# A gated DeltaNet layer with MLP on one core: down products over eight PSUM banks, up products moved between the token norms

## The chip, the core and the metric

The kernel runs on one core of a Trainium2 chip. The core has four compute engines, each with its own in-order queue of instructions: TensorE (PE: matmuls and transposes; PEld is its weight load), VectorE (DVE), ScalarE (ACT) and GpSimd (POOL). SyncE (SP) and ScalarE issue the DMAs. Engines wait for each other through semaphores. The metric is the device time of one execution in microseconds, and of several runs the median.

## The reference

One layer of a hybrid decoder over 2048 tokens of 1024 float32 features: a gated DeltaNet mixer, then a squared-ReLU MLP with 4096 hidden features, then the final norm.

```python
h = rms_norm(x, norm_mix[0])
x = x + gated_deltanet(h, ...)                       # 8 heads of 128
x = x + squared_relu_mlp(rms_norm(x, norm_mlp[0]), w_up, w_down)
return rms_norm(x, norm_final)

def squared_relu_mlp(h, w_up, w_down):
    return jnp.square(jax.nn.relu(h @ w_up)) @ w_down
```

## The kernel before

**Precision.** A float32 operand is split into a high and a low part. A product is then three matmuls, high by high, low by high and high by low, added up in one PSUM bank: lines 119, 120 and 121 in `dense`. So everything that enters a product is first cast (high) and subtracted (low).

**Stages.** The tokens are handled in two blocks of TB = 1024. Each block goes through the mixer, then `mlp_up`, then `mlp_down`. The tile framework takes the program as written, and its own scheduler decides the order in which each engine gets its instructions; a tile pool with `bufs=n` gives a name n buffers in turn, and whoever wants the next buffer waits for the last reader of what was in it.

**PSUM.** There are eight banks of 128x512 float32. They are shared out in three groups, `banks = dict(pj=3, kq=3, po=2)` (line 86), and `big(tag)` takes the next bank of a group.

**`mlp_up`.** The hidden features are made in tiles of 128 by 1024 tokens. `h2` holds the normalized tokens, features first, in two halves of HB = 512 tokens; the first is there when the stage begins, the second is made here. `part(w, u, hf)` is a plain product: 24 matmuls into a pj bank for one weight tile and one half, then relu and square on ScalarE (lines 742 and 743). Three of them on the first half (lines 761 and 762) stand ahead of the token norms. The norms then take the four tiles of 128 tokens in two pairs (`norm_pair`, loop at 788): VectorE scales a tile (line 218) into half of a `qt` buffer, whose other half a DMA fills with a normalized tile of the first half (`place`, line 772). `sums` (775 to 786) transposes on TensorE into kq banks (`to_features`, line 205, with the cast 207 on ScalarE and the subtraction 208 on VectorE), and makes four differences of quarters on GpSimd (lines 780, 782, 784 and 786), which are transposed too: they feed the fast products (`fast`, 835 to 868), in which seven products of half depth do the work of eight. `qt` has two buffers in its group, but `t4` holds one of them, so that the four tiles of tokens pass through a single one. Line 782 overwrites what the first transposes of a tile read. Behind the norms come the three products on the second half (790) and a fourth pair, then the fast products, which put their results in pj, kq and po banks in turn and write the hidden features to memory.

**`mlp_down`.** Sixteen calls of `down` a block, each for FT = 2 tiles of hidden features. `load(fb)` fetches two tiles u, casts them (uh, line 889, ScalarE) and subtracts (ul, line 890, VectorE, 128x1024 each), and splits two tiles of w_down on GpSimd (lines 92 and 93, called dh and dl or the two halves of w). `down` makes sixteen products, eight tiles of tokens by two halves of the features, of six matmuls each; every product is added to x1 by VectorE (line 915). The load of the next call is written ahead of the products of this one. All the products go to kq banks. The last call of a block adds the final norm (921 to 928) and writes the output through DMAs of two queues. In block 0 the call before the last is interleaved with `first_half`, which normalizes and transposes tokens of the next block through pj banks (lines 182 to 192).

Of the kernel before, what the change touches and what calls it, by code (L numbers as in the profile page):

```python
# [7 lines left out]
F32 = mybir.dt.float32  # L8
# [4 lines left out]
MULT, ADD, SUB = ALU.mult, ALU.add, ALU.subtract  # L13
# [7 lines left out]
TB = 1024  # L21
NT = TB // P
HB = 512
# [10 lines left out]
def tile_kernel(ctx: ExitStack, tc: tile.TileContext, x, w_in, w_out, w_up, w_down, n_mlp, n_fin, consts, out):  # L34
# [3 lines left out]
    pe, act, dve, pool, sp = nc.tensor, nc.scalar, nc.vector, nc.gpsimd, nc.sync  # L38
# [49 lines left out]
    def big(tag):  # L88
        return pp.tile([P, 512], F32, name=tag, tag=tag, bufs=banks[tag])
# [9 lines left out]
    def weights(src, f=1, keep=None):  # L99

        raw = wp.tile([P, D], F32, name="wr", tag="wr", bufs=2)
        sp.dma_start(raw if f == 1 else raw.rearrange("p (f c) -> p f c", f=f), src)
        w2, wh, wl = parts()
        split(wh, wl, raw)
        if keep is not None:
            sp.dma_start(keep, w2.bitcast(F32))
        return wh, wl
# [6 lines left out]
    def dense(ps, lhs, rhs, first=True, last=True):  # L114

        n = len(lhs)
        for i in range(n):
            (ah, al), (bh, bl) = lhs[i], rhs[i]
            pe.matmul(ps, ah, bh, start=first and i == 0, stop=False)  # L119
            pe.matmul(ps, al, bh, start=False, stop=False)  # L120
            pe.matmul(ps, ah, bl, start=False, stop=last and i == n - 1)  # L121

    def half_tiles():
        hh = hp.tile([P, KS, HB], F32R, name="hh", tag="hh")
        hl = hp.tile([P, KS, HB], F32R, name="hl", tag="hl")
        return hh, hl
# [16 lines left out]
    def rstd_of(ssq, use_pool=False):  # L143

        n = ssq.shape[-1]
        m = sm.tile([P, n], F32, name="rm", tag=f"rm{n}")
        dve.tensor_scalar(m, ssq, 1.0 / D, EPS, op0=MULT, op1=ADD)
        r = sm.tile([P, n], F32, name="rst", tag=f"rst{n}", bufs=3)
        if use_pool:
            pool.tensor_tensor(r, m, mhalf, op=ALU.pow)  # L150
        else:
            rsqrt(r, m)
        return r
# [47 lines left out]
    def to_features(ti, src, dst_h, dst_l):  # L201

        ps = big("kq")
        for k in range(4):
            pe.transpose(ps[:, k * P:(k + 1) * P], src[:, k * P:(k + 1) * P], ident)
        p3 = ps.rearrange("p (k t) -> p k t", k=4)
        act.copy(dst_h[:, :, ti], p3)
        dve.tensor_tensor(dst_l[:, :, ti], p3, dst_h[:, :, ti].bitcast(F32), op=SUB)

    def norm_pair(i0, xs, ss, place, nb, hh, hl, sums):  # L210


        ssq = sm.tile([P, 2], F32, name="ssq2", tag="ssq2")
        dve.tensor_reduce(ssq, ss, axis=mybir.AxisListType.X, op=ADD)
        r = rstd_of(ssq)
        for i in range(2):
            xn = place()
            dve.scalar_tensor_tensor(xn, xs[i], r[:, i:i + 1], nb, op0=MULT, op1=MULT)
            ti = slice((i0 + i) * P, (i0 + i + 1) * P)
            for k4 in range(0, KS, 4):  # L220
                to_features(ti, xn[:, k4 * P:(k4 + 4) * P], hh[:, k4:k4 + 4, :], hl[:, k4:k4 + 4, :])
            sums(i0 + i, xn)
# [495 lines left out]
    def mlp_up(blk, o1, x1b, h2a):  # L718
# [6 lines left out]
        with tc.tile_pool(name="mp", bufs=2) as mp:  # L725
# [12 lines left out]
            def u_tile():  # L738
                return wp.tile([P, TB], F32, name="u", tag="xt", bufs=4)

            def relu2(dst, src, r):
                act.activation(r, src, AF.Relu)
                act.activation(dst, r, AF.Square)

            def part(w, u, hf):
                (wh, wl), (hh, hl) = w, h2[hf]
                ps = big("pj")
                dense(ps, [(wh[:, k * P:(k + 1) * P], wl[:, k * P:(k + 1) * P]) for k in range(KS)],
                      [(hh[:, k, :], hl[:, k, :]) for k in range(KS)])
                r = mp.tile([P, HB], F32, name="r", tag="r", bufs=3)  # L750
                relu2(u[:, hf * HB:(hf + 1) * HB], ps, r)
                if hf:
                    return u

            def store(f, u):
                act.dma_start(u_d[f], u)


            ws = [weights(w_up[f]) for f in range(3)]
            us = [u_tile() for f in range(3)]  # L760
            for f in range(3):
                part(ws[f], us[f], 0)
            h2.append(half_tiles())
            t_h = [mp.tile([P, KH, HB], F32R, name=f"th{j}", bufs=1) for j in range(3)]
            t_l = [mp.tile([P, KH, HB], F32R, name=f"tl{j}", bufs=1) for j in range(3)]
# [21 lines left out]

            for i in range(0, HT, 2):
                norm_pair(i, x1b[i:i + 2], ss[i // 2], place, nb, *h2[1], sums)
            for f in range(3):  # L790
                store(f, part(ws[f], us[f], 1))
            w, u = weights(w_up[3]), u_tile()
# [83 lines left out]
    def mlp_down(blk):  # L876

        with tc.tile_pool(name="xp", bufs=1) as xp, tc.tile_pool(name="mq", bufs=2) as mp:
            x1 = [xp.tile([P, D], F32, name=f"x1_{i}") for i in range(NT)]
            nfb = DFF // (P * FT)  # L880

            def load(fb):
                us, ds = [], []
                for j in range(FT):
                    f = fb * FT + j
                    raw = wp.tile([P, TB], F32, name="u", tag="xt", bufs=4)
                    sp.dma_start(raw, u_d[f])
                    uh, ul = [mp.tile([P, TB], F32R, name=n, tag=n, bufs=2 * FT) for n in ("uh", "ul")]
                    act.copy(uh, raw)  # L889
                    dve.tensor_tensor(ul, raw, uh.bitcast(F32), op=SUB)  # L890
                    us.append((uh, ul))
                    raw = wp.tile([P, D], F32, name="wr", tag="wr", bufs=2)
                    sp.dma_start(raw, w_down[f * P:(f + 1) * P, :])
                    if j:
                        _, dh, dl = parts()
                    else:
                        dh, dl = [mp.tile([P, D], F32R, name=n, tag=n) for n in ("dh", "dl")]
                    split(dh, dl, raw)
                    ds.append((dh, dl))
                return us, ds  # L900

            def down(us, ds, last, after=None):
                if last:
                    nfin = mp.tile([P, D], F32, name="nfin", tag="nfin", bufs=1)
                    sp.dma_start(nfin, n_fin.to_broadcast([P, D]))
                for i in range(NT):
                    if last:
                        ssq = sm.tile([P, 2], F32, name="ssqf", tag="ssqf")
                    for nh in range(2):
                        ps = big("kq")  # L910
                        hs = slice(nh * 512, (nh + 1) * 512)
                        dense(ps, [(uh[:, i * P:(i + 1) * P], ul[:, i * P:(i + 1) * P]) for uh, ul in us],
                              [(dh[:, hs], dl[:, hs]) for dh, dl in ds])
                        dst = x1[i][:, hs]
                        dve.tensor_tensor(dst, ps, dst, op=ADD)  # L915
                        if last:
                            y = wp.tile([P, HB], F32, name="yo", tag="xt", bufs=4)
                            act.activation(y, dst, AF.Square, accum_out=ssq[:, nh:nh + 1])
                    if last:
                        m = sm.tile([P, 1], F32, name="mf", tag="mf")  # L920
                        dve.tensor_tensor(m, ssq[:, 0:1], ssq[:, 1:2], op=ADD)
                        r = rstd_of(m, True)
                        r0 = blk * TB + i * P
                        for nh in range(2):
                            hs = slice(nh * 512, (nh + 1) * 512)
                            dve.scalar_tensor_tensor(x1[i][:, hs], x1[i][:, hs], r, nfin[:, hs],
                                                     op0=MULT, op1=MULT)
                            (sp, act)[nh].dma_start(out[r0:r0 + P, hs], x1[i][:, hs])
                    if after:
                        after(i)  # L930

            prev, hT = load(0), None
            for i in range(NT):
                sp.dma_start(x1[i], x1_d[blk * TB + i * P:blk * TB + (i + 1) * P, :])
            for fb in range(1, nfb):
                cur = load(fb)
                after = None
                if fb == nfb - 1 and blk + 1 < nblk:
                    hT = half_tiles()
                    after = first_half(blk + 1, hT)  # L940
                down(*prev, False, after)
                prev = cur
            down(*prev, True)
            return hT

# [82 lines left out]
```

## Time and profile before

| | |
|---|---|
| runs | 2955.99, 2963.18 and 2971.45 us (median 2963.18) |
| the profiled execution | 2953.64 us |
| its span | 2951.9 us |
| mean granted TensorE clock | 0.966 |
| PE, DVE, ACT, POOL busy | 93%, 58%, 36%, 33% of the span |

The profile is a trace of one execution. A row of a timeline has the start in us, the duration in us, the engine, the line of the kernel, the operation, the output and inputs by the program's names, and in brackets how long the engine had been idle and what ended that. A row of a window has its bounds and length, the busy time of PE, PEld, DVE, ACT and POOL with the number of instructions, then the granted TensorE clock as a share of full speed, and the share and rate of the DMA engines. A row of waits has who waited, for whom, the total in us, how often, and the longest. A matmul is shown for longer than the distance to the next one, since they are pipelined: what a matmul costs is read from start to start.

### The profile page before, as it was taken

The page shows a single profiled execution, that of the slowest core. Times are in us where ns is not written, and L with a number is a line of the kernel's source. Part 1 is how long each engine was busy: PE and PEld are TensorE (multiplying, and loading weights), DVE is VectorE, ACT ScalarE, POOL GpSimd, SP SyncE. Part 2 cuts the span into 40 slices and gives each one's busy share as a digit, 9 for nine tenths or more (in the row PEclk, how much of TensorE's full clock was granted, in tenths as well). Part 3 has the DMA queues.
Part 4 walks back from the last instruction along what each step waited for, and adds up shares of the span by engine and source line. Part 5 has one row for each costly group of instructions (what it writes and reads, how often), then busy time and mean ns, then how long its engine had stood idle before and what let it go on. Part 6 is the DMA issues. An engine that isn't in the chain of part 4 may idle for free.

```text
span 2951.9 us, 39239 instructions
## 1 busy us (share of the span) xinstructions
PE 2754.7 (93%) x14376; PEld 2243.1 (76%) x14376; DVE 1710.1 (58%) x3978; ACT 1048.7 (36%) x2382; POOL 961.9 (33%) x790
## 2 busy tenths in 40 slices
PE   7788999999899998999999999999998999999998
PEld 6567778877778886777777778887786888777776
DVE  7887777764422225666688776776442222366666
ACT  3343444443244441000045554545423444200001
POOL 5443222200276763232211111111016766333221
PEclk9898999999999999999999999999998999999999
DMA  6544455566423235222254434435572323522221
GB/s 225 187 164 156 160 193 179 179 216 229 162 100 114 100 114 201 86 86 87 78 179 166 147 131 151 151 136 175 194 245 72 111 103 114 207 93 86 86 92 58
DMA packets 101681, 421.46 MB, mean 143 GB/s; under 512 B 11248, under 2 KB 11504, under 8 KB 79984
## 3 DMA queue, kind: packets, MB, share of 16 engines
q1 hardware_dynamic: 70000, 334.92, 32.9%
q10 hardware_dynamic: 31488, 84.03, 7.8%
q8 instruction: 113, 1.85, 0.3%
q14 instruction: 80, 0.66, 0.1%
HBM read 313.92 MB, written 104.99 MB: 142 GB/s over the span
## 4 chain that ended last, share of the span: by engine, by line
PE 70%; DVE 16%; ACT 5%; issue 5%; POOL 2%; DMA 1%; ACTq 0%; DVEq 0%; POOLq 0%; SPq 0%
PE kq L119 9%; PE kq L121 9%; PE kq L120 9%; PE pj L119 9%; PE pj L121 9%; PE pj L120 9%; DVE c L314 3%; DVE tmp L339 2%; PE po L119 2%; PE po L121 2%; PE po L120 2%; DVE ul L890 1%; DVE tt L341 1%; PE kq L517 1%; PE kq L511 1%
## 5 line engine op out<-in xcount | busy, mean ns | idle before, releaser
L119 PE MATMUL pj<-hh,w 128*128 128x512 f32 x1376 | 562.6, 409 | 0.0
L120 PE MATMUL pj<-hh,w 128*128 128x512 f32 x1376 | 557.1, 405 | 0.0
L121 PE MATMUL pj<-hl,w 128*128 128x512 f32 x1376 | 555.0, 403 | 0.0
L915 DVE TENSOR_TENSOR x<-kq,x 128x512 f32<-128x512 f32 x512 | 347.5, 688 | 267.0 <-PE kq L121 266.2
L121 PEld LDWEIGHTS pj<-hl,w 128*128 128x128 f32 x1376 | 265.1, 193 | 54.2 <-issue 0.4
L119 PEld LDWEIGHTS pj<-hh,w 128*128 128x128 f32 x1376 | 266.0, 193 | 51.7 <-issue 0.7
L120 PEld LDWEIGHTS pj<-hh,w 128*128 128x128 f32 x1376 | 266.3, 194 | 50.3
L314 DVE SCALAR_TENSOR_TENSOR c<-raw,cst,c 128x512 f32<-128x512 f32 x288 | 244.8, 855 | 72.7 <-ACT c L311 60.4
L889 ACT CAST uh<-u 128x1024 fp32r<-128x1024 f32 x64 | 64.1, 1046 | 623.9 <-PE kq L121 573.4
L92 POOL TENSOR_SCALAR w<-wr 128x1024 fp32r<-128x1024 f32 x80 | 86.6, 1082 | 513.2 <-PE po L121 312.9
L119 PE MATMUL kq<-dh,uh 128*128 128x512 f32 x512 | 206.4, 404 | 47.8 <-DVE x L915 40.4
L120 PE MATMUL kq<-dh,ul 128*128 128x512 f32 x512 | 204.7, 400 | 0.8 <-DVE ul L890 0.8
L121 PE MATMUL kq<-dl,uh 128*128 128x512 f32 x512 | 202.2, 395 | 2.8 <-POOL dl L93 2.8
L119 PE MATMUL kq<-w,uh 128*128 128x512 f32 x512 | 204.2, 399 | 0.0
L121 PE MATMUL kq<-w,uh 128*128 128x512 f32 x512 | 204.1, 399 | 0.0
L120 PE MATMUL kq<-w,ul 128*128 128x512 f32 x512 | 202.5, 395 | 0.0
L93 POOL TENSOR_TENSOR w<-wr,w 128x1024 fp32r<-128x1024 f32 x80 | 195.6, 2445 | 4.4
L339 DVE TENSOR_TENSOR tmp<-tt,pr 128x2 f32<-128x2 f32 (+30 forms) x496 | 164.6, 332 | 10.1 <-POOL pr L332 0.5
L92 POOL TENSOR_SCALAR dh<-wr 128x1024 fp32r<-128x1024 f32 x32 | 33.5, 1049 | 400.8 <-PE kq L120 349.6
L119 PEld LDWEIGHTS kq<-dh,uh 128*128 128x128 f32 x512 | 96.5, 189 | 82.8 <-DVE x L915 52.8
L890 DVE TENSOR_TENSOR ul<-u,uh 128x1024 fp32r<-128x1024 f32 x64 | 137.4, 2182 | 5.8 <-ACT uh L889 5.8
L341 DVE TENSOR_REDUCE tt<-tmp 128x1 f32<-128x2 f32 (+30 forms) x496 | 126.1, 254 | 10.0
(372 smaller groups left out, 5577.9 us busy)
## 6 DMA issues: line engine op xcount, KB each, us to landing
w<-wi SPq DMA_DIRECT2D x96, 1024.0 KB, 4.9
wi<-w SPq DMA_DIRECT2D x32, 1024.0 KB, 4.8
wr<-in_w_up SPq DMA_DIRECT2D x64, 512.0 KB, 3.6
w<-wo SPq DMA_DIRECT2D x32, 1024.0 KB, 5.8
u<-u ACTq DMA_DIRECT2D x64, 512.0 KB, 2.8
wr<-in_w_down SPq DMA_DIRECT2D x64, 512.0 KB, 3.5
u<-u SPq DMA_DIRECT2D x64, 512.0 KB, 4.7
wr<-in_w_in SPq DMA_DIRECT2D x32, 512.0 KB, 5.7
```

Source lines behind the costliest of these rows:

```text
L92: pool.tensor_scalar(dst_h, src, 1.0, 0.0, op0=MULT, op1=ADD)
L93: pool.tensor_tensor(dst_l, src, dst_h.bitcast(F32), op=SUB)
L119: pe.matmul(ps, ah, bh, start=first and i == 0, stop=False)
L120: pe.matmul(ps, al, bh, start=False, stop=False)
L121: pe.matmul(ps, ah, bl, start=False, stop=last and i == n - 1)
L314: dve.scalar_tensor_tensor(dst, raw[:, k:k + HB], cw[:, 4 * f + k:4 * f + k + 1], dst, op0=MULT, op1=ADD)
L339: dve.tensor_tensor(tmp[:, 0:n, 0:i + 1], tt[:, 0:n, 0:i + 1], pr[:, i, 0:i + 1].unsqueeze(1).to_broadcast([P, n, i + 1]), op=MULT)
L341: dve.tensor_reduce(tt[:, 0:n, i], tmp[:, 0:n, 0:i + 1], axis=mybir.AxisListType.X, op=ADD)
L511: pe.matmul(ps[:, 0:P], u["ub"][:, c, :], ys[j], start=True, stop=True)
L889: act.copy(uh, raw)
L890: dve.tensor_tensor(ul, raw, uh.bitcast(F32), op=SUB)
L915: dve.tensor_tensor(dst, ps, dst, op=ADD)
```

## The change

The diff has three parts. In `mlp_up` one plain product stays ahead of the norms; the second is written behind the first pair of tiles of tokens, the third behind the second pair. In `load` each ul is made in two pieces of 512 columns. In `down` the product of tile i and half nh takes its bank from a sequence of five names, over all three groups.

```diff
             ws = [weights(w_up[f]) for f in range(3)]
             us = [u_tile() for f in range(3)]
-            for f in range(3):
-                part(ws[f], us[f], 0)
+            part(ws[0], us[0], 0)
             h2.append(half_tiles())
...
             for i in range(0, HT, 2):
                 norm_pair(i, x1b[i:i + 2], ss[i // 2], place, nb, *h2[1], sums)
+                part(ws[1 + i // 2], us[1 + i // 2], 0)
             for f in range(3):
                 store(f, part(ws[f], us[f], 1))
...
                     act.copy(uh, raw)
-                    dve.tensor_tensor(ul, raw, uh.bitcast(F32), op=SUB)
+                    for hs in (slice(0, HB), slice(HB, TB)):
+                        dve.tensor_tensor(ul[:, hs], raw[:, hs], uh[:, hs].bitcast(F32), op=SUB)
                     us.append((uh, ul))
...
                     for nh in range(2):
-                        ps = big("kq")
+                        ps = big(("kq", "pj", "kq", "pj", "po")[(2 * i + nh) % 5])
                         hs = slice(nh * 512, (nh + 1) * 512)
```

Behind line 890 the new program's lines are one higher (the additions are line 916, the scalings of the final norm 927); between 762 and 786 they are one lower. What the scheduler makes of it is read from the order of instructions on each engine.

TensorE, block 0 of `mlp_up`, around the norms; `w_7278`, `w_7283` and `w_7288` are the first, second and third weight tile, and `qt` feeds the transposes. Before, the last rows of the third product and the start of the second half:

```order
L120 MATMUL pj<-hh,w_7288 128x512
L121 MATMUL pj<-hl,w_7288 128x512
L205 MATMUL kq<-cst,qt 128x128 x68
L119 MATMUL pj<-hh,w_7278 128x512
L205 MATMUL kq<-cst,qt 128x128 x4
L120 MATMUL pj<-hh,w_7278 128x512
L205 MATMUL kq<-cst,qt 128x128 x4
```

Now, the last rows of the first product and the start of the second:

```order
L120 MATMUL pj<-hh,w_7278 128x512
L121 MATMUL pj<-hl,w_7278 128x512
L205 MATMUL kq<-cst,qt 128x128 x12
L119 MATMUL pj<-hh,w_7283 128x512
L120 MATMUL pj<-hh,w_7283 128x512
L121 MATMUL pj<-hl,w_7283 128x512
L205 MATMUL kq<-cst,qt 128x128 x4
L119 MATMUL pj<-hh,w_7283 128x512
L120 MATMUL pj<-hh,w_7283 128x512
L205 MATMUL kq<-cst,qt 128x128 x4
```

The transposes began behind 72 matmuls of plain products, 68 in a row; now the first twelve stand behind 24, and the other two products lie between the groups of transposes. The orders of GpSimd and SyncE are the same there.

VectorE, the end of one call of `down` and the start of the next. Before:

```order
L915 TENSOR_TENSOR x_6_9690<-kq,x_6_9690 128x512 x2
L915 TENSOR_TENSOR x_7_9691<-kq,x_7_9691 128x512 x2
L890 TENSOR_TENSOR ul<-u,uh 128x1024 x2
L915 TENSOR_TENSOR x_0_9684<-kq,x_0_9684 128x512 x2
L915 TENSOR_TENSOR x_1_9685<-kq,x_1_9685 128x512 x2
```

Now:

```order
L916 TENSOR_TENSOR x_7_9691<-po,x_7_9691 128x512
L916 TENSOR_TENSOR x_7_9691<-kq,x_7_9691 128x512
L891 TENSOR_TENSOR ul<-u,uh 128x512 x4
L916 TENSOR_TENSOR x_0_9684<-kq,x_0_9684 128x512
L916 TENSOR_TENSOR x_0_9684<-pj,x_0_9684 128x512
L916 TENSOR_TENSOR x_1_9685<-kq,x_1_9685 128x512
L916 TENSOR_TENSOR x_1_9685<-pj,x_1_9685 128x512
L916 TENSOR_TENSOR x_2_9686<-po,x_2_9686 128x512
```

The additions keep their order and read from three groups of banks; the four pieces of ul stand in one row, where the two whole ones stood.

VectorE, the end of the last call of block 0, with the final norm (mf and rm are its mean, the scalings by rst and nfin its end). Before:

```order
L921 TENSOR_TENSOR mf<-ssqf 128x1
L915 TENSOR_TENSOR x_6_9690<-kq,x_6_9690 128x512
L147 TENSOR_SCALAR rm<-mf 128x1
L915 TENSOR_TENSOR x_6_9690<-kq,x_6_9690 128x512
L926 SCALAR_TENSOR_TENSOR x_5_9689<-x_5_9689,rst,nfin 128x512 x2
```

Now:

```order
L916 TENSOR_TENSOR x_1_9685<-pj,x_1_9685 128x512
L916 TENSOR_TENSOR x_3_9687<-pj,x_3_9687 128x512
L916 TENSOR_TENSOR x_4_9688<-pj,x_4_9688 128x512
L922 TENSOR_TENSOR mf<-ssqf 128x1
L147 TENSOR_SCALAR rm<-mf 128x1
L927 SCALAR_TENSOR_TENSOR x_1_9685<-x_1_9685,rst,nfin 128x512 x2
L922 TENSOR_TENSOR mf<-ssqf 128x1
L916 TENSOR_TENSOR x_5_9689<-pj,x_5_9689 128x512
L147 TENSOR_SCALAR rm<-mf 128x1
```

Before, each tile was added and scaled in turn. Now the additions from pj banks, which the transposes of the next block's tokens use too, stand behind those from kq and po, and the scalings of all the tiles follow at the end. On TensorE the projections of the next mixer, of which some stood between the last products, now all follow them; in that mixer the rows of all engines are ordered anew.

## The prediction

> **What bounds the kernel now.** I began with the busy shares and the chain that ended last, then took windows by stage, then the waits of TensorE in the two stages that the diff touches.
>
> ```profile
> span 2951.9 us, 39239 instructions
> PE 2754.7 (93%) x14376; PEld 2243.1 (76%) x14376; DVE 1710.1 (58%) x3978; ACT 1048.7 (36%) x2382; POOL 961.9 (33%) x790
> PE 70%; DVE 16%; ACT 5%; issue 5%; POOL 2%; DMA 1%; ACTq 0%; DVEq 0%; POOLq 0%; SPq 0%
> ```
>
> TensorE is busy 93% of the span and leads the chain. It is idle for 2951.9 − 2754.7 = 197 us in all; no change that leaves its matmuls alone can win more than that, plus what a halved clock costs. Where in the stages of this diff does the idle time lie?
>
> ```profile
> core 0: us, PE busy (x) PEld busy (x) DVE busy (x) ACT busy (x) POOL busy (x), PEclk, DMA share, GB/s
> 776.00:793.00 17.00, 17.00 (x78) 14.03 (x77) 9.36 (x29) 3.28 (x7) 4.75 (x3) 1.00 0.31 99
> 793.00:826.00 33.00, 20.78 (x93) 15.37 (x92) 17.22 (x23) 13.27 (x23) 19.09 (x15) 0.64 0.15 48
> 860.00:1120.00 260.00, 260.00 (x1124) 210.91 (x1123) 64.71 (x94) 114.62 (x168) 171.85 (x101) 1.00 0.32 112
> 1160.00:1500.00 340.00, 319.80 (x1373) 254.05 (x1372) 220.08 (x305) 36.21 (x53) 95.12 (x54) 1.00 0.25 84
> ```
>
> These are block 0. The three plain up products (776 to 793) fill TensorE; the token norms behind them (793 to 826) leave it 12.2 us idle, and the granted clock falls; the fast products (860 to 1120) fill it fully; the down products (1160 to 1500) lose 20.2 us. What ends the waits of the last window is one line, and over both blocks the page has the same releaser:
>
> ```profile
> PE kq L119 <- DVE x L915: 20.2, 14, 2.1
> L119 PE MATMUL kq<-dh,uh 128*128 128x512 f32 x512 | 206.4, 404 | 47.8 <-DVE x L915 40.4
> ```
>
> Fourteen waits in block 0, and 40.4 / 20.2 says as many in block 1: one in each of the down calls 1 to 14, 28 in all. A single one, by engine:
>
> ```profile
> 1254.05 0.69 DVE L915 TENSOR_TENSOR x<-kq,x 128x512 f32<-128x512 f32 x1 [0.71 <-PE kq L121]
> 1254.65 4.27 DVE L890 TENSOR_TENSOR ul<-u,uh 128x1024 fp32r<-128x1024 f32 x2
> 1258.85 1.87 DVE L915 TENSOR_TENSOR x<-kq,x 128x512 f32<-128x512 f32 x3
> 1278.64 4.27 DVE L890 TENSOR_TENSOR ul<-u,uh 128x1024 fp32r<-128x1024 f32 x2
> 1254.30 2.40 POOL L93 TENSOR_TENSOR dl<-wr,dh 128x1024 fp32r<-128x1024 f32 x1
> 1255.24 0.39 PE L119 MATMUL kq<-dh,uh 128*128 128x512 f32 x1
> 1256.64 0.40 PE L119 MATMUL kq<-dh,uh 128*128 128x512 f32 x1
> 1257.80 0.39 PE L121 MATMUL kq<-w,uh 128*128 128x512 f32 x1
> 1259.58 0.50 PE L119 MATMUL kq<-dh,uh 128*128 128x512 f32 x1 [1.39 <-DVE x L915]
> ```
>
> VectorE works off an addition as each product ends, then spends 4.27 us on two low parts of u (the first runs beside GpSimd's 2.40 us). Meanwhile TensorE fills its three kq banks, one product of six matmuls each 1256.64 − 1255.24 = 1.40 us, and stands until an addition at 1258.85 ends. VectorE then makes up three additions in a row: it has slack, only not at that moment. So a kq bank is what TensorE lacks, for some 1.7 us a call.
>
> **The down products, part by part.** Six matmuls in 1.40 us are 0.233 each; a call of 96 is 22.34 us. The ul pairs stand at 1254.65 and 1278.64: a call takes 23.99. So a stall costs 23.99 − 22.34 = 1.65 us. The first stall of a block is longer:
>
> ```profile
> 1163.63 0.50 PE L119 MATMUL kq<-dh,uh 128*128 128x512 f32 x1 [2.11 <-DVE x L915]
> ```
>
> A wait of 2.11 us against 1.39, so 1.65 + 0.72 = 2.37. The new sequence of banks uses a bank again after six products or more (kq, the tightest: products 10, 12 and 15 of a call, then 0, 2 and 5 of the next), 6 × 1.40 = 8.4 us. VectorE's block lasts 4.27 and the additions behind it 1.87 for three; the first bank comes free some 5 us after its product ended, so every one of these stalls should vanish, with 3 us to spare. What is late next? VectorE's work per call is 4.27 + 16 × 0.62 (1.87 / 3) = 14.2 us of 22.3, and GpSimd is busy 95 of the window's 340 us; neither binds.
>
> The pieces of 512 do not land between additions: the order has all four in a row where two stood. Their cost:
>
> ```profile
> L560 DVE TENSOR_TENSOR hl<-orw,hh 128x512 fp32r<-128x512 f32 x32 | 21.8, 688 | 39.9 <-ACT hh L559 39.8
> L890 DVE TENSOR_TENSOR ul<-u,uh x64: 1209/1658/3415, 1128.8 to 2900.3; 128x1024 fp32r<-128x1024 f32 x64
> ```
>
> The same subtraction with 512 columns takes 0.688 us, twice 1.376 against 1.209 alone: at most 4 × 0.17 = 0.7 us more a call, and by the sum of two pairs at least nothing. That lies in VectorE's 8 us of slack; without the new banks it would lengthen each stall, to 28 × 0.7 = 19 us. I take nothing.
>
> Block 1: 2.37 + 13 × 1.65 = 23.8 us. Block 0 has another end: its last two calls share the pj banks and VectorE with the transposes of the next block's tokens.
>
> ```profile
> L926 DVE SCALAR_TENSOR_TENSOR x<-x,rst,nfin 128x512 f32<-128x512 f32 x32 | 22.7, 748 | 4.0 <-POOL rst L150 2.8
> 1527.94 6.24 DMA out<-x
> 1534.40 0.58 ACT raw L310
> ACT raw L310 <- DMA out<-x: 9.7, 1, 9.7
> ```
>
> The second and third rows are from the chain of 1470 to 1545, the last from its waits: after the last scaling by the final norm the next mixer waits 6.24 us for the last output DMA, since its first copy reuses that memory. So the stall at 1473 is hidden under this end, and I count 12 of 13: 2.37 + 12 × 1.65 = 22.2 us. The new order puts the pj additions and all scalings of eight tokens at the very end: 16 × 0.748 = 12.0 us of VectorE in one row, their 16 output DMAs bunched. Meanwhile TensorE can do only three projections, one a pj bank: 72 matmuls, at 0.233 some 16.8 us. Against 12.0 + 6.24 = 18.2 us that leaves TensorE idle 1.5 us or so more. The DMAs themselves may take longer: were all sixteen stretched to twice the 6.24, 6 us more; were the old end kept, nothing. I take −2 us, from −6 to +1.65 (the 14th stall gained as well).
>
> At the start of each block's down stage the product of the second bank no longer stands ahead of a wait; I charge two matmuls (2 × 0.233) a block, 0.9 us in all. **Down: 22.2 − 2 + 23.8 − 0.9 = 43.1 us.**
>
> **The up products between the norms.**
>
> ```profile
> 783.32 1.29 POOL L780 TENSOR_TENSOR qt<-qt 128x512 f32<-128x512 f32 x1 [2.96 <-DVE ssq L214]
> 793.63 1.27 POOL L782 TENSOR_TENSOR qt<-qt 128x512 f32<-128x512 f32 x1 [9.01 <-PE kq L205]
> 801.21 1.27 POOL L780 TENSOR_TENSOR qt<-qt 128x512 f32<-128x512 f32 x1 [3.60 <-PE kq L205]
> 810.19 1.27 POOL L780 TENSOR_TENSOR qt<-qt 128x512 f32<-128x512 f32 x1 [3.67 <-PE kq L205]
> 2220.46 1.27 POOL L782 TENSOR_TENSOR qt<-qt 128x512 f32<-128x512 f32 x1 [9.02 <-PE kq L205]
> 795.02 0.63 PE L205 MATMUL kq<-cst,qt 128*128 128x128 f32 x4 [0.67 <-POOL qt L782]
> 799.65 0.52 PE L205 MATMUL kq<-cst,qt 128*128 128x128 f32 x3 [2.68 <-DVE qt L218]
> 823.18 1.03 PE L205 MATMUL kq<-cst,qt 128*128 128x128 f32 x4
> qt<-xn_d SPq DMA_DIRECT2D x3, 512.0 KB, 3.4
> ```
>
> The four tokens are a chain with a period of 8.98 us (801.21 to 810.19): four GpSimd operations of 1.27, then a DMA of 3.4 us into the one free quarter buffer. All that could have begun at 783.32 + 1.29: L782 waits 9.0 us, in both blocks, for transposes that stand behind three products in TensorE's order. In the new order twelve of them stand behind one product, so L782 can run at 783.32 + 1.29 + 0.04 = 784.65, that is 793.63 − 784.65 = 8.98 us earlier, and all behind it moves by as much: the chain is the same, on the same engines. TensorE meanwhile has 48 matmuls for its gaps; by the end of the transposes (824.21 before) it has done all three products and two matmuls of the next half, where before it had done three. At full clock the last four transposes take 0.63 us (795.02), not 1.03: 0.4 us less; one matmul less is −0.23. 8.98 + 0.4 − 0.23: **9.15 us a block, 18.3 in all.** ScalarE now does the two operations of a product (L742, L743) between the casts L207; it was busy 13.27 of 33 us there, so that hides in its gaps, and if a cast comes late by one such operation in each token, 4 × 0.6 = 2.4 us a block are gone. The whole idle time of the stage, 12.2 + what the halved clock costs, is not to be had: the DMA and GpSimd become the bound there.
>
> That rests on the clock:
>
> ```profile
> 798.00:800.00 2.00, 0.35 (x3) 0.38 (x4) 1.51 (x2) 0.41 (x1) 0.00 (x0) 1.00 0.65 172
> 800.00:802.00 2.00, 1.19 (x7) 0.79 (x5) 0.85 (x2) 1.39 (x3) 0.79 (x1) 0.52 0.23 90
> 800.00:824.00 24.00, 15.80 (x63) 11.39 (x61) 11.77 (x16) 9.05 (x16) 14.78 (x12) 0.50 0.15 52
> ```
>
> Before, it fell after a stretch in which TensorE was busy 0.35 of 2 us, and stayed at 0.50 until 824. In the new order the longest gap that I work out is under 2 us. Were it to fall all the same, the 48 matmuls would take 48 × 0.23 = 11 us more; half of that has room in the gaps, so 5 us a block are lost, 10 in all. [...]
>
> **The sum.** 43.1 + 18.3 = 61.4 us, off the profiled execution's 2953.64 (span 2951.9): 2892. The median of the runs, 2963.18, lies 9.5 above that one; from it 2902. Behind block 0 the mixer of block 1 is ordered anew by the scheduler on every engine.
>
> ```profile
> 110.00:700.00 590.00, 531.65 (x3488) 443.04 (x3487) 427.18 (x1236) 274.65 (x766) 148.97 (x164) 0.93 0.50 174
> 1534.00:2124.00 590.00, 565.57 (x3731) 472.80 (x3730) 424.11 (x1411) 304.59 (x836) 64.85 (x137) 0.97 0.43 152
> ```
>
> Its idle time there is 24.4 us, and in block 0, under another order, 58.3. I take no change, with −10 and +15 us as ends: a little under half of the idle, and a little under half of the difference.
>
> **The rivals.**
> - *Only part comes.* The pj banks tie the two last calls to the transposes, and the new mixer order is worse: the tail costs 6 and not 2, the mixer 15, the clock falls (10). 61.4 − 4 − 15 − 10 = 32 us: 2931. For it: the bunched rows at the end, and block 0's mixer. Against: TensorE is busy there in both orders.
> - *More comes.* The whole idle of the norms goes (12.2 and about 9 us of half clock in each block, so 2 × 21 = 42 instead of 18.3) and the mixer gains: some 2870. Against it stands the DMA period of 8.98 us.
> [...]
> - *The change does not do what it says.* For the pieces this is certain: they stay in a row, and give nothing. For the banks it can't be: the order has the tags in turn.
>
> **How the numbers follow.** The forecast (2880 to 2920) has 0.68, only part 0.18, more 0.10, slower 0.02, and 0.02 for a reordered mixer that eats nearly all. The range leaves out 2 in 10: 2876 to 2931, which takes in the unknown ends (below, the mixer's 10 and half of the further gain in the norms; above, the 32 us of the rival in part). About 0.5% (15 us) is what a measurement of this kernel can tell from no change. Faster by more 0.95, within 0.03, slower 0.02.
>
> **What would show it.** Right: no wait of L119 for the addition in calls 1 to 14, a call of 22.3 us; L782 within 1.5 us of L780 and the last L205 of the norms some 9 us earlier at a granted 1.00; ul x4 in 4.3 to 5 us on VectorE. Wrong: waits of TensorE for pj additions in calls 14 and 15, an output DMA that ends the tail later than before, a granted clock below 1.00 between the norms, or more than 30 us of idle time in block 1's mixer.

## The result and the profile after

The changed kernel takes 2914.88 us (median of 4 runs, 2912.83 to 2918.48) against 2959.59 us before: a ratio of 0.9844, 95% interval 0.9811 to 0.9877. Timed once more beside the experiments it took 2905.44 against 2956.13 us, 0.9833 (0.9819 to 0.9847). So it is faster by 45 to 51 us. The forecast was 61 us less, 2902, in a range of 2876 to 2931.

The page of the changed kernel, its span and TensorE's busy time:

```profile
span 2916.7 us, 39352 instructions
PE 2748.9 (94%) x14376; PEld 2246.7 (77%) x14376; DVE 1723.5 (59%) x4042; ACT 1049.3 (36%) x2382; POOL 959.3 (33%) x790
```

The stalls of the down products are gone. The window of block 0's down calls in the changed kernel, and VectorE's timeline at two boundaries of calls there:

```profile
core 0: us, PE busy (x) PEld busy (x) DVE busy (x) ACT busy (x) POOL busy (x), PEclk, DMA share, GB/s
1145.00:1450.00 305.00, 305.00 (x1312) 246.01 (x1311) 207.50 (x275) 29.05 (x30) 99.39 (x57) 1.00 0.29 95
```

```profile
1246.02 4.41 DVE L891 TENSOR_TENSOR ul<-u,uh 128x512 fp32r<-128x512 f32 x4
1252.75 0.67 DVE L916 TENSOR_TENSOR x<-po,x 128x512 f32<-128x512 f32 x1
1268.37 4.41 DVE L891 TENSOR_TENSOR ul<-u,uh 128x512 fp32r<-128x512 f32 x4
```

TensorE is busy 305.00 of 305 us at a granted clock of 1.00. A call takes 1268.37 − 1246.02 = 22.35 us, where it took 23.99; 22.34 were forecast. VectorE still spends 4.41 us on ul and then makes up five additions in a row, but nobody waits for it.

Where the whole time went is read from starts in the trace: the first matmul L119 of w by hh into a pj bank, which begins the out projection (653.85 and 2080.29 us before), the first product of the down stage (1128.91, 2555.70), ScalarE's first copy in block 1's mixer (1534.40) and TensorE's end. In us, with the difference to before:

| from one start to the next | before | after | after, again | forecast |
|---|---|---|---|---|
| block 0: mixer, to the out projection | 653.85 | +1.60 | −2.47 | 0 |
| block 0: out projection to down stage | 475.06 | −4.67 | −5.02 | −9.15 |
| block 0: down stage to first copy of next mixer | 405.49 | −11.63 | −12.26 | −19.7 |
| block 1: mixer, to the out projection | 545.89 | +6.55 | −3.72 | 0 |
| block 1: out projection to down stage | 475.41 | −5.09 | −3.06 | −9.15 |
| block 1: down stage to the end | 387.47 | −22.18 | −22.10 | −23.3 |
| sum | 2943.17 | −35.42 | −48.63 | −61.4 |

The two columns of the changed kernel are two executions of one program. In the four stages that the change touches they agree within 0.7 us, but for block 1's norms, which differ by 2 us; in block 1's mixer they differ by 10 us. An order can't be the reason for that, since it is the same in both. The mixer of block 0, too, is the same program in all kernels of this study, and ended between 647.47 and 663.70 us in their traces. So a stage is read from its own segment, and a total from medians of several runs.

What is missing against the forecast lies in the norms (9 to 10 us in both blocks together) and in the stretch with the end of block 0 (7 to 8 us).

**The norms.** The changed kernel in block 0, GpSimd first, then TensorE, then VectorE:

```profile
785.07 1.27 POOL L779 TENSOR_TENSOR qt<-qt 128x512 f32<-128x512 f32 x1 [2.96 <-DVE ssq L214]
786.41 1.29 POOL L781 TENSOR_TENSOR qt<-qt 128x512 f32<-128x512 f32 x1
787.79 1.26 POOL L783 TENSOR_TENSOR qt<-qt 128x512 f32<-128x512 f32 x1
798.39 1.28 POOL L779 TENSOR_TENSOR qt<-qt 128x512 f32<-128x512 f32 x1 [8.00 <-DMA qt<-xn_d]
```

```profile
786.39 0.66 PE L205 MATMUL kq<-cst,qt 128*128 128x128 f32 x4 [0.29 <-POOL qt L779]
791.94 1.09 PE L205 MATMUL kq<-cst,qt 128*128 128x128 f32 x4 [4.20 <-DVE hl L208]
793.68 1.05 PE L205 MATMUL kq<-cst,qt 128*128 128x128 f32 x4
```

```profile
785.04 0.17 DVE L147 TENSOR_SCALAR rm<-ssq 128x2 f32<-128x2 f32 x1
785.24 1.12 DVE L132 TENSOR_SCALAR rh<-rm 128x2 f32<-128x2 f32 x1
786.47 1.26 DVE L139 TENSOR_TENSOR rt<-rst 128x2 f32<-128x2 f32 x1
787.96 1.11 DVE L141 SCALAR_TENSOR_TENSOR rst<-rt,rst 128x2 f32<-128x2 f32 x1
790.64 0.16 DVE L139 TENSOR_TENSOR rt<-rst 128x2 f32<-128x2 f32 x1
791.10 1.28 DVE L208 TENSOR_TENSOR hl<-kq,hh 128x512 fp32r<-128x512 f32 x2
798.19 1.29 DVE L208 TENSOR_TENSOR hl<-kq,hh 128x512 fp32r<-128x512 f32 x2 [1.46 <-ACT hh L207]
```

The same small operations of VectorE before the change (three of them):

```profile
783.49 1.15 DVE L132 TENSOR_SCALAR rh<-rm 128x2 f32<-128x2 f32 x1
784.74 0.16 DVE L139 TENSOR_TENSOR rt<-rst 128x2 f32<-128x2 f32 x1
786.31 0.16 DVE L141 SCALAR_TENSOR_TENSOR rst<-rt,rst 128x2 f32<-128x2 f32 x1
```

L781 (L782 before the change) does run right behind L779, the wait of 9 us is gone. But the second tile's L779 comes at 798.39, 13.3 us after the first, and not 9.0. VectorE computes the inverse root of the second pair of tiles at just this time, in thirteen operations, nearly all on 128x2, which take 0.16 us alone. Four of them met an operation of GpSimd and ended with it: L132 at 786.36, as L779 at 786.34; L139 at 787.73, as L781 at 787.70; L141 at 789.07, as L783 at 789.05; L140 at 790.41, as L785 at 790.39. So the subtractions L208, which stand behind them in VectorE's order and free the three kq banks, begin only at 791.10; TensorE waits 4.20 us for a bank; and the transposes of the last quarter (793.68), after which the DMA may refill `qt`, are late by as much. Before the change only L132 met a GpSimd operation; the rest ran while GpSimd was the one that waited (from 784.6 to 793.63), and the row of thirteen took 3.4 us, where it now takes 6.3. Behind TensorE's wait the granted clock fell, in the window from 790 on:

```profile
790.00:795.00 5.00, 3.06 (x12) 2.70 (x13) 3.70 (x10) 0.82 (x2) 0.39 (x1) 0.68 0.00 0
```

Not every operation of VectorE was held up: L208, which has one of its two inputs in PSUM, took the same beside a GpSimd operation (two in 1.29 us from 798.19, beside L779 from 798.39) as without one (two in 1.28 us from 791.10; GpSimd's last operation had ended at 790.39). What makes the small operations end with GpSimd's, the traces don't show.

**The end of block 0.** The changed kernel, from the chain of work, and two windows:

```profile
1509.07 0.56 POOL rst L150
1509.66 1.42 DVE x L927 x2
1511.47 0.56 POOL rst L150
1512.06 1.43 DVE x L927 x2
1513.51 5.90 DMA out<-x
1519.70 0.58 ACT raw L310
1520.29 0.59 ACT c L311
1520.88 0.46 ACT bat L239
1521.38 1.89 PE po L243 x8
```

```profile
1510.00:1520.00 10.00, 4.93 (x22) 3.75 (x20) 2.71 (x6) 0.30 (x1) 0.78 (x2) 0.94 1.00 377
1520.00:1530.00 10.00, 8.62 (x26) 7.16 (x27) 6.17 (x16) 4.38 (x10) 3.39 (x9) 0.55 0.07 29
```

The scalings come in pairs, one pair a tile of tokens, and each of the last pairs waits for an inverse root that GpSimd computes from a mean just made: nothing is left to fill these waits. TensorE's last down product and VectorE's last two scalings, in the changed kernel and then before:

```profile
1499.25 0.39 PE L121 MATMUL pj<-w,uh 128*128 128x512 f32 x1
1512.06 1.42 DVE L927 SCALAR_TENSOR_TENSOR x<-x,rst,nfin 128x512 f32<-128x512 f32 x2 [0.73 <-POOL rst L150]
```

```profile
1522.74 0.39 PE L121 MATMUL kq<-w,uh 128*128 128x512 f32 x1
1526.49 1.42 DVE L926 SCALAR_TENSOR_TENSOR x<-x,rst,nfin 128x512 f32<-128x512 f32 x2 [0.73 <-POOL rst L150]
```

So the scalings end 14.0 us behind the last product (its last matmul costs 0.22 us), where they ended 5.0 us behind it: 9 us later. The output DMA behind them is no longer than before, 5.90 us against 6.24. The mixer's first copy waits for it, and there the stretch ends. What follows counts in the mixer's row: ScalarE's copies; the idle time of TensorE, which has done three projections by then and stands 6.44 us in front of L243; and a granted clock of 0.50 from 1520 to 1529.

```profile
1521.38 1.89 PE L243 MATMUL po<-cst,bat 32*128 32x16 f32 x8 [6.44 <-ACT bat L239]
```

### The profile page after: what moved, and what is told of

It reads as the page before. It is cut to its first block, busy times and chain, and to the rows that moved or that the text cites. A ratio compares the mean times of both kernels' runs of the same rounds, so it can differ in the third digit from the quotient of the medians.

```text
span 2916.7 us, 39352 instructions
## 1 busy us (share of the span) xinstructions
PE 2748.9 (94%) x14376; PEld 2246.7 (77%) x14376; DVE 1723.5 (59%) x4042; ACT 1049.3 (36%) x2382; POOL 959.3 (33%) x790
## 4 chain that ended last, share of the span: by engine, by line
PE 73%; DVE 15%; ACT 5%; DMA 2%; issue 2%; POOL 2%; ACTq 0%; POOLq 0%; DVEq 0%; SPq 0%
PE pj L119 11%; PE pj L120 11%; PE pj L121 11%; PE kq L120 6%; PE kq L121 6%; PE kq L119 6%; DVE c L314 3%; PE po L119 3%; PE po L121 3%; PE po L120 3%; DVE tmp L339 3%; DVE tt L341 1%; PE kq L517 1%; PE kq L511 1%; PE kq L502 1%
## 5 line engine op out<-in xcount | busy, mean ns | idle before, releaser
L119 PE MATMUL pj<-hh,w 128*128 128x512 f32 x1376 | 565.0, 411 | 0.0
L119 PEld LDWEIGHTS pj<-hh,w 128*128 128x128 f32 x1376 | 267.8, 195 | 51.9 <-issue 0.6
L916 DVE TENSOR_TENSOR x<-kq,x 128x512 f32<-128x512 f32 x224 | 153.7, 686 | 95.1 <-PE kq L121 94.9
L916 DVE TENSOR_TENSOR x<-pj,x 128x512 f32<-128x512 f32 x192 | 131.5, 685 | 85.6 <-PE pj L121 85.6
L891 DVE TENSOR_TENSOR ul<-u,uh 128x512 fp32r<-128x512 f32 x128 | 148.7, 1219 | 5.8 <-ACT uh L889 5.8
L308 POOL COPY raw<-tail 128x3 f32<-128x3 f32 x96 | 19.8, 207 | 319.8 <-DVE c L318 146.0
L317 ACT ACTIVATE raw<-c 128x512 f32<-128x512 f32 x96 | 60.6, 632 | 153.1 <-DVE c L314 101.8
L850 DVE TENSOR_TENSOR r<-kq,r 128x512 f32<-128x512 f32 x28 | 19.4, 693 | 137.5 <-PE kq L121 118.2
L513 ACT ACTIVATE vr<-kq,cc 128x128 f32<-128x128 f32 x128 | 45.5, 367 | 153.2 <-PE kq L511 141.6
L821 POOL TENSOR_TENSOR w<-s,w 128x1024 fp32r<-128x1024 f32 x28 | 67.4, 2407 | 98.0 <-ACT w L820 98.0
L119 PE MATMUL kq<-dh,uh 128*128 128x512 f32 x224 | 89.1, 398 | 7.4 <-ACT uh L889 7.4
```

Of the source, the lines that this page charges most:

```text
L821: pool.tensor_tensor(o[:, 1, :], src, o[:, 0, :].bitcast(F32), op=SUB)
L891: dve.tensor_tensor(ul[:, hs], raw[:, hs], uh[:, hs].bitcast(F32), op=SUB)
```

## The experiments

The first four ran on one chip beside 2956.62 us of before, the next four beside 2956.13, the last two beside 2958.91. For each the three segments that the change touches are given as "norms" (blocks 0 and 1), "down 0" (to the next mixer's first copy) and "down 1", as differences to before.

**Only the up products moved** (banks and ul as before):

> Only the up products are moved; banks (kq alone) and whole ul as before. In the changed kernel's trace the norms gave some 4.7 us in block 0 and 5.1 in block 1, not 9.15 each. If the two other parts have nothing to do with it, this kernel is 9 to 11 us faster than before (ratio 0.9965), its first GpSimd operation of the second tile comes 13.3 us behind that of the first, and VectorE's 28 waits of the down stage stay (40 us). A rival, by which the norms' own shortfall came from how the changed kernel was otherwise scheduled: 18 us faster, and the distance is 9 us.

2948.67 us, ratio 0.9964 (0.9948 to 0.9981): 8 us less by the medians, 10.6 by the ratio. Norms −4.97 and −4.92, down 1 +0.93. The second tile's first GpSimd operation is at 799.46, 13.2 us behind 786.25, and the waits stay:

```profile
PE kq L119 <- DVE x L915: 40.8, 29, 2.1
```

The shortfall in the norms is there with this part of the change alone.

**Only the banks changed:**

> Only the banks of the down products are changed; ul whole, up products as before. Theory: the stalls go in both blocks, 22 us from each down stage, and the end of block 0 gives back 12 to 17 us between its last calls and the mixer of block 1, so 27 to 32 us faster than before. A rival, that what was given back there comes from the moved up products or the pieces: 44 us faster. A second: that without the pieces VectorE's block is shorter and the gain in each down stage larger, 25 us a block.

2915.08 us, ratio 0.9851 (0.9821 to 0.988): 42 us less by the medians, 44 by the ratio, and not the 27 to 32 of the theory, which let the end of block 0 give back 12 to 17. The total is that of the first rival, but not for its reason: down 0 is −13.77, 11 us less than down 1, so the end gives back nearly as much without the other two parts. That trace's first mixer was 6.38 us short by itself. Down 1 is −25.10, 3 us better than in the changed kernel: the second rival, and the reason to test the pieces.

**Five banks, none of pj:**

```diff
-                        ps = big(("kq", "pj", "kq", "pj", "po")[(2 * i + nh) % 5])
+                        ps = big(("kq", "po", "kq", "po", "kq")[(2 * i + nh) % 5])
```

> The changed kernel, with the down products in the five banks of kq and po and none in pj. Theory: pj products in the two last calls of block 0 are what delays its end (they share the pj banks with the transposes of the next block's tokens, so the scheduler puts them, their additions, all the scalings and the next mixer's projections at the end). Without them the order of the end is as before, and 8 to 14 us more are won than by the changed kernel; a bank is used again after five products, 7.0 us less one product, against some 5 to 5.5 us until VectorE has read it, so no stall comes back. A rival, that the order of block 1's mixer is what costs: no difference to the changed kernel within 4 us. A second, that five banks are too few: waits of 0.3 to 0.8 us in each of 28 calls, 10 to 20 us of the gain lost.

2907.79 us, ratio 0.982 (0.98 to 0.984). Down 0 −18.40, 6 to 7 us better than with pj, where the theory had 8 to 14; down 1 −20.38, some 2 us worse: one stall of 1.7 us comes back in each block, which the theory had excluded, and no other. Five banks are enough for the rest. The total, against 0.9844 and 0.9833 of the changed kernel, doesn't settle the end by itself.

**The roots of all four tiles at once:**

```diff
+            ssq4, m4, r4 = [mp.tile([P, HT], F32, name=n, bufs=1) for n in ("ssq4", "m4", "r4")]
+            for i in range(2):
+                dve.tensor_reduce(ssq4[:, 2 * i:2 * i + 2], ss[i], axis=mybir.AxisListType.X, op=ADD)
+            dve.tensor_scalar(m4, ssq4, 1.0 / D, EPS, op0=MULT, op1=ADD)
+            rsqrt(r4, m4, mp, bufs=1)
             for i in range(0, HT, 2):
-                norm_pair(i, x1b[i:i + 2], ss[i // 2], place, nb, *h2[1], sums)
+                norm_pair(i, x1b[i:i + 2], None, place, nb, *h2[1], sums, r4[:, i:i + 2])
```

> The changed kernel, with the roots of both pairs of token tiles taken at once (128x4) ahead of the first tile, so that the thirteen small VectorE operations of the second pair are gone. Theory: these, stretched to 1.1 us and more beside GpSimd's operations, held up the subtractions that free the kq banks (TensorE waited 4.20 us); without them the first GpSimd operation of the second tile follows that of the first after 9 to 9.5 us instead of 13.3, and the norms end 3.5 to 4.4 us sooner in each block, less up to 0.7 us for a later start: 6 to 8 us faster than the changed kernel in all. A rival, that the three kq banks or the lower clock at 790 to 795 us are the cause: the distance stays above 12 us and the time within 2 us of the changed kernel's.

2905.42 us, ratio 0.9813 (0.9791 to 0.9835). GpSimd in its trace, the first and the second tile (its line 780 is the changed kernel's 779):

```profile
787.32 1.27 POOL L780 TENSOR_TENSOR qt<-qt 128x512 f32<-128x512 f32 x1 [3.53 <-DVE qt L219]
796.25 1.26 POOL L780 TENSOR_TENSOR qt<-qt 128x512 f32<-128x512 f32 x1 [3.57 <-DMA qt<-xn_d]
```

8.93 us, the period of the chain that the prediction had taken for all the tiles. Norms −8.99 and −7.32. All traces say the same: in the six with the products moved and the roots as before, this distance is 13.2 to 13.4 us in both blocks; in the four with the roots taken at once (this one and three below) it is 8.9 to 9.1; the two distances behind it are 8.8 to 9.0 in every trace. The clock is not the cause of the longer distance, since it fell in this kernel too, only later (a row of TensorE, then three windows):

```profile
797.57 0.65 PE L205 MATMUL kq<-cst,qt 128*128 128x128 f32 x4 [1.25 <-POOL qt L780]
```

```profile
797.00:800.00 3.00, 1.31 (x8) 0.83 (x8) 0.69 (x1) 0.98 (x2) 2.84 (x3) 1.00 0.00 0
800.00:805.00 5.00, 4.75 (x16) 4.01 (x17) 2.58 (x3) 2.00 (x4) 1.47 (x2) 0.66 0.31 105
801.00:803.00 2.00, 2.00 (x7) 1.61 (x6) 0.98 (x2) 0.58 (x1) 0.55 (x1) 0.50 0.17 31
```

The small operations were the cause. And the clock fell although TensorE's longest gap before it was 1.25 us: it was busy 1.31 of 3 us from 797 to 800, in short pieces. The prediction had counted on the full clock with gaps that it put at under 2 us, an estimate of its author; here it fell behind gaps of 1.25 us at most.

**The changed kernel again:**

> The changed kernel itself, timed beside the next three and profiled once more. By the traces so far the first mixer, which is the same program everywhere, began its last products between 647 and 657 us; so a single trace is uncertain by some 5 us at each mixer. Theory: the norms of both blocks and the down stage of block 1 repeat within 1 us (4.7 + 5.1 and 22.2 us won), the stretch from block 0's first down product to the first copy of the next mixer repeats within 2 us (11.6 us won), and only the mixers differ. A rival: that stretch, too, differs from execution to execution by 5 us or more, and nothing is to be explained there.

2905.44 us, ratio 0.9833 (0.9819 to 0.9847). The table above has its segments: block 0's norms and both down stages repeat within 0.7 us, block 1's norms only within 2 (the theory had 1), the mixers within some 4 and 10.

**ul whole again** (the loop over two pieces undone):

> The changed kernel with ul made whole again. Theory: the pieces cost time only at the start of each down stage, where the third and fourth wait out a second GpSimd subtraction (7.25 us for four pieces against 4.94 for two whole ones) while TensorE waits for them; without them its wait for ul falls from 2.7 to 0.4 us in each block, and the time by 4 to 5 us. A rival, that the pieces lengthen VectorE's block in every call and nothing hides that: 15 us or more. A second, that they do nothing: within 1.5 us.

2905.51 us, ratio 0.9827 (0.9804 to 0.985): no difference in the time that these runs can tell. By the time alone it is the second rival; the segments speak for the theory: down 1 is −24.68 and down 0 −14.91, 2.5 to 3.3 us better each than with the pieces. The first low parts of a down stage, in the changed kernel and then here:

```profile
1125.73 7.25 DVE L891 TENSOR_TENSOR ul<-u,uh 128x512 fp32r<-128x512 f32 x4 [2.88 <-ACT uh L889]
```

```profile
1125.97 4.95 DVE L890 TENSOR_TENSOR ul<-u,uh 128x1024 fp32r<-128x1024 f32 x2 [2.88 <-ACT uh L889]
```

Four pieces take 2.3 us longer than two whole ones there; TensorE's wait for ul is 2.7 us with them and 0.9 without.

**The last two calls of block 0 in kq alone:**

> The changed kernel, with the last two calls of block 0 in kq banks alone, as before the change. Theory: the pj products of these calls are what makes block 0 end late; without them the order of the end is as before, TensorE has projections between the last products and no 6.4 us wait in front of the next mixer, and the stretch to the mixer's first copy is shorter by 4 to 8 us, less some 2 to 3 us for a stall in these two calls: 3 to 6 us faster than the changed kernel. A rival, that the end is bound by VectorE whichever banks are used: the same within 2 us.

2904.78 us, ratio 0.9829 (0.981 to 0.9847): the same as the changed kernel, by the time. Its segment is not: down 0 −20.37, 8 to 9 us better, with one stall of 1.5 us in it; the last scaling ends 5.0 us behind the last product again. In this trace the mixer behind it was 4.34 us longer than before, which is within what the mixers differ anyway. The time alone would have spoken for the rival, so the question was put once more, below.

**All together**, with kq and po in the last two calls of block 0:

> The changed kernel with all that the runs so far speak for: ul whole, the roots of the four token tiles at once, and in the last two calls of block 0 the five banks of kq and po; the other calls keep the eight banks. Theory: the gains add up, 6 to 7 us from the roots, 4 to 5 from the pieces, 6 to 8 from the end of block 0: 16 to 20 us faster than the changed kernel, 2890 to 2900. A rival, that what is won in the norms or at the end of block 0 is lost again in the mixer of block 1, which the scheduler orders anew: less than 10 us.

2889.78 us, ratio 0.9778 (0.9753 to 0.9803), 16 us less than the changed kernel beside it: the lower end of the theory. Norms −8.80 and −9.13, down 0 −23.09, down 1 −24.63. The last scaling ends 8.0 us behind the last product. TensorE's waits from 1430 to 1520 us, which hold the end of block 0, are two, against 6.4 and 3.1 us in the changed kernel (there to 1530, since its end is later):

```profile
PE pj L188 <- DVE xn L183: 1.3, 1, 1.3
PE po L244 <- ACT bat L240: 1.1, 1, 1.1
```

**The same, with pj in the last two calls, and the same again:**

> The kernel of the run best with one thing undone: its last two calls of block 0 take the eight banks again, pj among them. The traces so far have block 0's stretch from the first down product to the next mixer's first copy 6 to 9 us shorter wherever those calls leave pj alone, but the time of tail_kq was no better than the changed kernel's. Theory: the stretch is 8 us longer than in best, and the time 5 to 9 us longer, 2895 to 2899. A rival, that the mixer behind it makes up for that: the stretch is 8 us longer, the mixer as much shorter, and the times lie within 2 us of each other.

> The kernel of the run best once more, beside best_pj_end on the same chip. Theory: 2886 to 2893 us, 64 to 70 us faster than before, with segments as in the first trace: 8.8 to 9.1 us won in each block's up stage, 23 in block 0's down stage with its end, 24.6 in block 1's. A rival, that the first trace was a lucky one: 2895 or more.

With pj at the end 2897.54 us, ratio 0.9788 (0.977 to 0.9806); without it 2887.65, ratio 0.976 (0.9736 to 0.9785). Down 0 is −14.65 and −23.24: 8.6 us, and the medians are 9.9 us apart, though the intervals overlap. The waits of the kernel with pj, from 1430 to 1530 us:

```profile
PE po L244 <- ACT bat L240: 6.0, 1, 6.0
PE pj L188 <- DVE xn L183: 3.0, 2, 1.6
```

They are those of the changed kernel again, and the last scaling ends 14.0 us behind the last product, as in all six traces with pj at the end; without pj it is 4.6 to 5.0 us where the last calls have kq alone and 8.0 where they have kq and po. So pj at the end costs 8 to 9 us of block 0's segment; that the time shows all of it is likely by the medians, and not proved.

The kernel with all three mends is 66 to 71 us faster than before in its two measurements.

## Why the prediction was right, and where it fell short

- **What bounded the down stage** (a kq bank, while VectorE made ul): right. All 28 stalls went, the call takes 22.35 us, and block 1 gave 22.1 of the 23.3 forecast. Without the pieces it gave 24.6 to 25.5 in five traces, a little more than the 23.8 counted for the stalls. VectorE's slack held.
- **The pieces**, "I take nothing": right for the calls with stalls, where ul takes 4.41 us against 4.27 and is hidden. (The bound of 0.7 us a call counts too much: two low parts a call at 0.17 us make 0.34.) At the start of each stage, where no cost of the pieces was foreseen, they cost 2.5 to 3.3: the third of four pieces took 2.84 us beside GpSimd's second subtraction (1129.02 to 1131.82), and the fourth, behind it, 0.68; of two whole ones, before the change, the second met that subtraction only for its last 1.1 us.
- **The norms**, 9.15 us a block: the step that failed is "the chain is the same, on the same engines". It took VectorE's work for given. That work had been hidden in the very wait that the change removed. With the chain started early, thirteen small operations fell beside GpSimd, took 6.3 us in place of 3.4 and held up the release of kq banks; 4.7 and 5.0 us were left in block 0, 5.1 and 3.1 in block 1. With them out of the way it was 6.7 to 9.1 us in the eight blocks of four traces, 8.8 or more in five of them; why three gave less was not looked for.
- **The clock** between the norms: it did fall, to 0.68 from 790 to 795. There it came behind the wait of 4.20 us, so it did not cause that wait. But it fell without such a wait, too, to 0.50 from 801 to 803, where the roots were taken at once, and there block 0's norms gave 8.99 of the 9.15 us all the same. That gaps under 2 us keep the full clock, as the 18.3 us took for granted, no run shows; little of the gain hung on it.
- **The end of block 0**, −2 us: the sign was right, the size was not; it is some 8 to 9 us, outside the −6 to +1.65 given. The prediction set 12.0 us of scalings and 6.24 of DMA against 16.8 of projections, and let the projections hide nearly all. The DMA was right (5.90). The scalings took 14.0 us behind the last product, since the waits for GpSimd's roots between them (0.73 us in front of each of the last three pairs) had been left out, and the stretch ends with them and the DMA whatever TensorE does meanwhile. ScalarE's copies, the 6.44 us of idle time and the granted clock of 0.50 behind them had been left out too, but they fall into the mixer. Where the end is mended the stretch gives 23.1 us, and the wait of call 14 is gone as well; how much of the 23.1 is that stall, which the prediction took for hidden, the traces don't show, since the order of the end is not quite that of before.
- **The mixer of block 1**, taken as 0 with ends of −10 and +15: two executions gave +6.55 and −3.72, no more than mixers differ anyway. A cost or gain of its new order can't be told from that.
- **Slower**, given 0.02, did not come: with the banks in turn TensorE was busy 305.00 of 305 us of the down stage at a granted clock of 1.00.
- The rival "only part comes" was the nearest one, and for one of its three reasons, the end of block 0. The clock fell as it said, but that is not what cost; the mixer shows nothing.

Most of the gain came where it was forecast to come. Two terms were too big, one since the early start met another engine, one since a change in banks also changed what the scheduler could place where. Both erred the same way, by some 17 us together, and nothing made up for it: the time lies in the range because the range was wide enough, not because the sum was right in each part.

## What to carry to other kernels

When a wait is removed, list what the other engines did during it: work that was hidden there is now beside whatever starts early, and here small operations of VectorE on SBUF took 1.1 to 1.26 us beside GpSimd's in place of 0.16. More PSUM banks in turn are worth having where one engine is late only in bursts (28 waits, 40.4 us, went here), but banks that another stage needs at the same time are not free (8 to 9 us of block 0's segment here): keep a shared group out of the calls in which the stages overlap. Where a stage's segment repeats to 1 or 2 us and the total scatters by 15 or more, judge an edit by its segment, and use the total to see that nothing behind gave it back.

## What the runs showed of the hardware

VectorE's operations on 128x2 took 0.16 us alone and 1.1 to 1.26 us beside GpSimd's subtractions, ending within 0.03 us of them; subtractions that read PSUM (0.65 to 0.69 us) were not held up: two took 1.29 us beside GpSimd and 1.28 without it. With the roots taken at once the granted clock fell to 0.50 behind 3 us in which TensorE was busy for 1.31, with no gap over 1.25 us. The mixer of block 0, one and the same program, took from 647 to 664 us in twelve traces: what decides that was not looked for.
